# An identity matrix made on Pool, and the first K row moved ahead of the second Q row in the opening of an attention kernel

## The chip, the cores and the metric

The kernel runs on one core of one Trainium2 chip. The metric is the device time of one execution in microseconds. Each time given for a kernel is the median of several runs; one further execution was recorded by the hardware profiler, and all rows of a profile come from it.

## The reference

```
d_k = q.shape[-1]                                   # q, k, v: 8 x 2048 x 512, float32
scores = np.matmul(q, k.transpose(0, 2, 1)) / np.sqrt(d_k)
attn_weights = special.softmax(scores, axis=-1).astype(np.float32)
return np.matmul(attn_weights, v)
```

Plain attention without a mask, for 8 batches of 2048 queries and keys of width 512.

## The kernel before

The kernel casts q, k and v to 16-bit floats, brings q and k into transposed form (width on the partitions), forms transposed score tiles with TensorE, puts them through an exponential on ScalarE, and multiplies the weights with v. Most products of both matmuls are done seven for eight, by a scheme of Strassen's kind; the sums that this needs are VectorE's work. The row sums come from a column of ones next to v. All instructions are issued in an order written by hand: each engine runs its own list in that order, and strings of words (`SECOND`, `OPENING`, `SEQUENCES`) say what comes next. In the steady state, q and k are loaded by Pool with a cast into `stage` and transposed by DMA from SP.

The change lies in the opening, the first dozen microseconds, where that way would be too slow to start. There the first four rows of Q blocks and of K blocks (a "row" here is a block of 128 queries or keys by 512 numbers, 256 KB as float32) are loaded without a cast, by `load_first`. Q row 0 goes first on SP's queue, K row 0 on ACT's queue (it is the only one there besides the identity), and Q row 1, K row 1, Q row 2, K row 2, Q row 3 and K row 3 follow on SP's. `round_first` casts a row to 16 bits: Q rows on VectorE (DVE), K rows on ScalarE (ACT). `first_transpose` then transposes it on TensorE (PE), by four 128x128 transposes against an identity matrix `ident` into a PSUM tile `tr`, which DVE copies into `qraw` or `kraw`. `piece(kb, half, n, w)` multiplies K block `kb` with `w` of the Q rows from `n` on. In the profile the load is line 131, the cast line 135, the transposes line 156, their copy line 159 and the product of `piece` line 258.

`ident` lies in a corner of the tile `vt4`, which is not needed for v before much later. It comes from a constant in DRAM by a DMA that ACT issues ahead of everything else (line 95). `idle(n, name, w)` issues `n` dummy matmuls of width `w` (512 by default) on a cleared tile `warm` (line 768); they fill PE's time while it has nothing to multiply.

Behind the first rows come the other rows of the first batch. Pool loads them (`LOADS`, ten words, in the order q1, k1, q2, k2, k3, v0, v1, q3, v2, v3, where each is four rows), some of them into the places `left` and `right` that the weights use later. So that they do not take the DMA engines from the first rows, Pool first runs a one-column copy into `gate`, which reads K row 0 (line 728) and so cannot start before that row has landed. PE transposes these rows too, in `OPENING`, for which `q10v`, `k20v`, `q30v` and so on are the words (line 156 again, reading `right` or `left`).

Of the kernel before, what the change touches and what calls it, by code (L numbers as in the profile page):

```python
# [12 lines left out]
def kernel(  # L13
# [21 lines left out]
    nc = tc.nc  # L35
    P = 128
# [37 lines left out]
    def bank(name):  # L74
        t = psum[name].tile([P, 512], F32, tag=name)
        return t
# [14 lines left out]
    vt4 = const.tile([P, NJ, H], F16, name="vt4")  # L91
    ident = vt4[:, NJ - 1, 0:P]
    warm = vt2[:, 0:2, :].rearrange("p j d -> p (j d)")
    ident_dram = nc.inline_tensor(np.eye(P, dtype=np.float16), name="attn_identity")
    nc.scalar.dma_start(out=ident, in_=ident_dram.ap())
    NK = NJ // 2
    Q = H // 2
    vus = [[const.tile([P, NK, Q], F16, name=f"vu{n}_{h}") for n in (1, 2, 4)] for h in range(2)]
# [25 lines left out]
    firsts = {}  # L124
# [8 lines left out]
    def round_first(what, n):  # L133
        f = nc.vector.tensor_copy if what == "q" else nc.scalar.copy
        f(out=staged[what, 0, 0][:, n, :], in_=firsts[what, n])  # L135
# [15 lines left out]
    def transposed(what, c, n, w, copy):  # L151
        src = staged[what, 0, c]
        tr = psum["px"].tile([P, 2, ND, P], F16, tag="px", name="tr")
        for m in range(w):
            for dc in range(ND):
                nc.tensor.transpose(  # L156
                    tr[:, m, dc, :], src[:, n + m, dc * P:(dc + 1) * P], ident
                )
        copy(out=raw_of(what, 0, c)[:, n:n + w], in_=tr[:, 0:w])  # L159
        if n + w == CH:  # L160
            staged.pop((what, 0, c))
# [5 lines left out]
    def first_transpose(what, n, copy=nc.vector.tensor_copy):  # L167
        transposed(what, 0, n, 1, copy)
# [59 lines left out]
    def weights(sp, kb, half):  # L228

        left, right = pts[sp]  # L230
        j, s = divmod(kb, 2)
        if half:
            return right[:, j, 1 + s, :]
        return right[:, j, 0, :] if s else left[:, j, :]

    def exp(out_, in_):
        nc.scalar.activation(out=out_, in_=in_, func=EXP, scale=inv_sqrt_d)  # L237
# [13 lines left out]
    def piece(kb, half, n, w, last=False):  # L251

        fresh = (kb, half) not in banks
        if fresh:
            banks[kb, half] = bank(HOMES[half][kb])
        st = banks[kb, half]
        for dc in range(ND):
            nc.tensor.matmul(  # L258
                st[:, n * P:(n + w) * P], kraw[:, kb, dc, :],
                qraw[0][:, half * NT + n:half * NT + n + w, dc, :],  # L260
                start=(fresh and dc == 0), stop=(dc == ND - 1), skip_group_check=True,
            )
        if last:
            exp(weights(0, kb, half), st[:])
# [442 lines left out]
    )  # L707

    nc.vector.memset(warm, 0.0)
    nc.gpsimd.memset(vt1[:, :, H:H + 1], 1.0)  # L710
    nc.gpsimd.memset(vraw[0][:, :, 1, D:D + 1], 1.0)

# [12 lines left out]
        load_first("k", n, nc.sync, rest[n])  # L725

    gate = const.tile([P, 1], F32)
    nc.gpsimd.tensor_copy(out=gate[:], in_=firsts["k", 0][:, 0:1])

    new_p(1)  # L730
    spare = [
# [34 lines left out]
    def idle(n, name="qy", w=512):  # L766
        for _ in range(n):
            nc.tensor.matmul(
                dummies[name][:, 0:w], warm[:, 0:P], warm[:, 0:w], start=True, stop=True
            )  # L770
# [3 lines left out]
    round_first("q", 0)  # L774
    round_first("k", 0)
    first_transpose("q", 0)
    round_first("q", 1)
    round_first("k", 1)
    idle(2)
    first_transpose("q", 1)  # L780
    idle(4, "pz", P)
    first_transpose("k", 0)
    idle(6, "pz", P)
    round_first("q", 2)
    round_first("k", 2)
    piece(0, 0, 0, 1)
    first_transpose("k", 1)
    piece(0, 0, 1, 1)
    first_transpose("q", 2)
# [95 lines left out]
```

## Time and profile before

| | before |
|---|---|
| median of 3 runs | 788.87 us |
| lowest and highest | 788.74 and 789.52 us |
| the profiled execution's own time | 790.05 us |
| its span, first to last instruction | 788.2 us |
| PE busy in the span | 782.7 us (99%) |
| DVE, ACT, Pool busy | 683.8, 609.8, 72.3 us |
| HBM read and written | 100.70 and 33.55 MB |

In rows of the timeline, the first number is the start in microseconds from the start of the span, the second the length; then come the engine, the line, the operation, what is written and what is read, the shape and the count. Square brackets hold the idle time before it and what ended it. PEld is TensorE's load of weights, which can run beside a matmul; an engine's name with a q behind it stands for its queue, where DMAs are issued. "DMA to landing" is the time from the issue of a DMA to its data being there. A busy PE is not PE at its peak, since the ends of matmuls are modelled.

### The profile page before, as it was taken

To read this page: it belongs to the slowest core of one execution; us is meant where nothing else is said; L and a number is where in the kernel's file an instruction comes from. 1 tells how busy PE (TensorE), PEld (TensorE's weight loads), DVE (VectorE), ACT (ScalarE), POOL (GpSimd) and SP (SyncE) were. 2 spreads that over 40 slices of the span, in tenths; PEclk is the share of its full clock that TensorE was granted. 3 is DMA by queue.
4 is the path that set the end of the run, shared out by engine and by line. 5 is a ranking of instruction groups with operands and counts; after the bars stand their busy time and mean duration, and the time that the engine had idled before them with its cause. 6 is when DMAs were issued, how large, how long until landed. Compare 5 with 4: busy or idle time off the path is not lost.

```text
span 788.2 us, 16289 instructions
## 1 busy us (share of the span) xinstructions
PE 782.7 (99%) x6284; PEld 536.4 (68%) x6284; DVE 683.8 (87%) x1452; ACT 609.8 (77%) x1140; POOL 72.3 (9%) x105
## 2 busy tenths in 40 slices
PE   8999999999999999999999999999999999999998
PEld 6566667667667666666666666666666766766677
DVE  5799988989889898998879988799897988889884
ACT  4888788787877878878787878878788777887762
POOL 4011100011000110010100001000110001100000
PEclk9999999999999999999999999999999999999999
DMA  9999895889958889589895989958898688921113
GB/s 210 190 155 167 155 182 125 164 149 151 198 114 162 156 150 175 110 162 179 119 193 126 160 161 146 191 108 169 141 191 155 117 178 137 191 75 45 48 67 110
DMA packets 187789, 115.90 MB, mean 147 GB/s; under 512 B 121536, under 2 KB 170816, under 8 KB 187712
## 3 DMA queue, kind: packets, MB, share of 16 engines
q0 software_dynamic: 49664, 49.29, 43.7%
q1 hardware_dynamic: 137616, 65.22, 36.8%
q8 instruction: 49, 0.80, 0.4%
q10 hardware_dynamic: 432, 0.36, 0.2%
q14 instruction: 28, 0.23, 0.1%
HBM read 100.70 MB, written 33.55 MB: 170 GB/s over the span
## 4 chain that ended last, share of the span: by engine, by line
PE 97%; DMA 2%; DVE 0%; ACT 0%; issue 0%; ACTq 0%; DVEq 0%
PE t L298 46%; PE t L494 36%; PE t L418 12%; DMA kraw<-stage 1%; PE t L243 1%; PE t L258 1%; PE tr L156 1%; DMA rows<-in_k_dram 1%; PE t L566 0%; DVE kraw L159 0%; ACT rows L435 0%; DVE rows L506 0%; DVE ks L185 0%; ACT stage L135 0%; DVE cz L318 0%
## 5 line engine op out<-in xcount | busy, mean ns | idle before, releaser
L298 PE MATMUL t<-qraw,kraw 128*128 128x512 f16 x732 | 192.4, 379 | 0.0
L494 PEld LDWEIGHTS <-s 128*128 128x128 f16 x1536 | 147.8, 98 | 39.4 <-ACT rows L503 0.3
L298 PEld LDWEIGHTS <-kraw 128*128 128x128 f16 x984 | 93.3, 98 | 79.0 <-issue 0.2
L298 PE MATMUL t<-qs,ks 128*128 128x512 f16 x492 | 141.1, 379 | 0.0
L494 PE MATMUL t<-vt,s 128*128 128x257 f16 (+1 forms) x1024 | 132.9, 273 | 0.0
L237 ACT ACTIVATE right<-cz 128x1024 f16<-128x1024 f32 x123 | 129.9, 1056 | 0.3 <-DVE cz L318 0.3
L426 DVE TENSOR_TENSOR rows<-t,rows 128x256 f32<-128x256 f32 x210 | 88.1, 419 | 22.3 <-ACT rows L517 11.8
L298 PEld LDWEIGHTS <-ks 128*128 128x128 f16 x738 | 69.3, 98 | 46.7 <-issue 0.2
L503 ACT ACTIVATE rows<-t,scales 128x256 f32<-128x256 f32 x136 | 63.9, 471 | 45.2 <-PE t L494 20.9
L506 DVE SCALAR_TENSOR_TENSOR rows<-t,scales,rows 128x256 f32<-128x256 f32 (+1 forms) x134 | 64.0, 479 | 34.4 <-ACT rows L503 21.0
L321 DVE TENSOR_TENSOR cz<-t,cz 128x512 f32<-128x512 f32 x123 | 84.2, 685 | 10.5 <-ACT cz L315 7.9
L237 ACT ACTIVATE left<-t 128x512 f16<-128x512 f32 x128 | 76.5, 598 | 20.1 <-PE t L298 16.3
L237 ACT ACTIVATE right<-t 128x512 f16<-128x512 f32 x138 | 83.1, 605 | 8.5 <-PE t L298 5.7
L318 DVE TENSOR_TENSOR cz<-t,cz 128x512 f32<-128x512 f32 x123 | 84.2, 684 | 4.4 <-PE t L298 3.8
L312 ACT COPY cz<-t 128x512 f32<-128x512 f32 x122 | 71.4, 585 | 15.7 <-PE t L298 13.5
L315 ACT COPY cz<-t 128x512 f32<-128x512 f32 x123 | 71.6, 582 | 10.3 <-PE t L298 10.0
L418 PEld LDWEIGHTS <-left 128*128 128x128 f16 x960 | 62.3, 98 | 23.3 <-DVE left L398 4.1
L308 ACT COPY t<-t 128x512 f32<-128x512 f32 x121 | 69.8, 577 | 6.3 <-PE t L298 4.0
L298 PE MATMUL t<-qraw,ks 128*128 128x512 f16 x246 | 73.2, 379 | 0.0
L298 PE MATMUL t<-qs,kraw 128*128 128x512 f16 x246 | 73.2, 379 | 0.0
L494 PE MATMUL t<-vh,right 128*128 128x256 f16 x544 | 69.8, 273 | 0.0
L494 PE MATMUL t<-vh,s 128*128 128x257 f16 x512 | 66.7, 273 | 0.1
(87 smaller groups left out, 1067.1 us busy)
## 6 DMA issues: line engine op xcount, KB each, us to landing
out_dram<-rows SPq DMA_DIRECT2D x60, 512.0 KB, 3.4
vh<-in_v_dram POOLq DMA_DIRECT2D x32, 512.0 KB, 10.8
stage<-in_q_dram POOLq DMA_DIRECT2D x28, 512.0 KB, 6.5
stage<-in_k_dram POOLq DMA_DIRECT2D x28, 512.0 KB, 7.2
right<-in_k_dram POOLq DMA_DIRECT2D x2, 512.0 KB, 12.1
out_dram<-rows SPq DMA_DIRECT2D x4, 256.0 KB, 2.0
out_dram<-rows SPq DMA_DIRECT2D x7, 128.0 KB, 1.7
rows<-in_q_dram SPq DMA_DIRECT2D x2, 256.0 KB, 3.3
```

What stands on the lines that cost most here:

```text
L237: nc.scalar.activation(out=out_, in_=in_, func=EXP, scale=inv_sqrt_d)
L298: nc.tensor.matmul(dst[:], lhs[:, j, dc, :], rhs[:, :, dc, :], start=(n in (1, 5) and dc == 0), stop=(dc == 1), skip_group_check=True,)
L308: self.edges[0](out=self.y[:], in_=self.x[:])
L312: self.edges[1](out=self.cz[:, 1, :], in_=self.z[:])
L315: nc.scalar.copy(out=self.cz[:, 0, :], in_=self.x[:])
L318: nc.vector.tensor_add(self.cz[:, 1, :], self.x[:], self.cz[:, 1, :])
L321: nc.vector.tensor_add(self.cz[:, 0, :], self.z[:], self.cz[:, 0, :])
L418: nc.tensor.matmul(to, lhs[:, j, h, :], rhs[:, j, :], start=(n in (1, 2) and h == 0 and j == 0), stop=(j == NK - 1), skip_group_check=True,)
L426: nc.vector.tensor_add(acc, part, acc)
L494: nc.tensor.matmul(dst[:, 0:width], lhs(j), rhs(j), start=(first and j == 0), stop=(j == NJ - 1), skip_group_check=True,)
L503: nc.scalar.activation(out=out_, in_=src, func=COPY, scale=r)
L506: nc.vector.scalar_tensor_tensor(out=out_, in0=src, scalar=r, in1=out_, op0=MULT, op1=ADD)
```

## The change

The identity is no longer loaded: Pool clears the 128x128 corner and then sets its diagonal to one by an `affine_select`, ahead of its two other memsets. ACT's first DMA is then K row 0. The gate of Pool's loads reads K row 1 instead of K row 0. In the opening's order, the transposes of K row 0 and the first product (`piece(0, 0, 0, 1)`) stand before the cast and transposes of Q row 1 and before the cast of K row 1, and the dummies are dealt out anew.

```diff
-    ident_dram = nc.inline_tensor(np.eye(P, dtype=np.float16), name="attn_identity")
-    nc.scalar.dma_start(out=ident, in_=ident_dram.ap())
...
     nc.vector.memset(warm, 0.0)
+    nc.gpsimd.memset(ident, 0.0)
+    nc.gpsimd.affine_select(
+        out=ident, in_=ident, compare_op=mybir.AluOpType.not_equal, fill=1.0,
+        base=0, pattern=[[-1, P]], channel_multiplier=1,
+    )
     nc.gpsimd.memset(vt1[:, :, H:H + 1], 1.0)
     nc.gpsimd.memset(vraw[0][:, :, 1, D:D + 1], 1.0)
...
     gate = const.tile([P, 1], F32)
-    nc.gpsimd.tensor_copy(out=gate[:], in_=firsts["k", 0][:, 0:1])
+    nc.gpsimd.tensor_copy(out=gate[:], in_=firsts["k", 1][:, 0:1])
...
     round_first("q", 0)
     round_first("k", 0)
     first_transpose("q", 0)
+    idle(1)
+    first_transpose("k", 0)
     round_first("q", 1)
     round_first("k", 1)
-    idle(2)
+    idle(4, "pz", P)
+    piece(0, 0, 0, 1)
+    idle(4, "pz", P)
     first_transpose("q", 1)
-    idle(4, "pz", P)
-    first_transpose("k", 0)
-    idle(6, "pz", P)
+    idle(2, "pz", P)
     round_first("q", 2)
     round_first("k", 2)
-    piece(0, 0, 0, 1)
     first_transpose("k", 1)
     piece(0, 0, 1, 1)
```

## The prediction

> **What bounds the kernel now.** The page comes first, for the engine that the chain of waits runs through.
>
> ```profile
> PE 782.7 (99%) x6284; PEld 536.4 (68%) x6284; DVE 683.8 (87%) x1452; ACT 609.8 (77%) x1140; POOL 72.3 (9%) x105
> PE 97%; DMA 2%; DVE 0%; ACT 0%; issue 0%; ACTq 0%; DVEq 0%
> ```
>
> PE is busy for 99% of the span and carries 97% of the chain. An edit that only reorders the opening can win what PE stands idle there, and no more. The windows view says where that idle time lies (columns: stretch, length, busy time and count of PE, PEld, DVE, ACT, POOL, granted clock, DMA share, GB/s).
>
> ```profile
> 0.00:9.12 9.12, 6.92 (x46) 3.49 (x46) 3.16 (x9) 3.09 (x5) 3.07 (x11) 1.00 0.74 237
> 9.12:60.00 50.88, 50.88 (x383) 31.89 (x384) 41.39 (x92) 38.73 (x67) 10.73 (x16) 1.00 1.16 176
> 60.00:400.00 340.00, 339.88 (x2718) 232.24 (x2717) 303.35 (x641) 270.63 (x510) 31.87 (x43) 1.00 0.88 155
> 400.00:780.00 380.00, 380.00 (x3089) 264.32 (x3088) 333.02 (x709) 296.03 (x557) 26.68 (x36) 1.00 0.72 135
> ```
>
> From 9.12 to 780 us PE is idle for 0.12 us of 770.88. Before 9.12 it is idle for 2.20, and part of its 6.92 busy is dummy matmuls. So whatever moves the matmul at 9.12 moves the end by as much, as long as nothing later holds PE up. The chain in order of time says what puts that matmul at 9.12 (start, length, what):
>
> ```profile
> 1.13 5.24 DMA rows<-in_k_dram
> 6.37 0.02 issue
> 6.39 0.63 ACT stage L135
> 7.02 0.05 issue
> 7.07 0.41 PE tr L156 x4
> ...
> 7.50 0.44 DVE kraw L159
> ...
> 8.38 0.24 PE tr L156 x4
> ...
> 8.64 0.43 DVE kraw L159
> 9.08 0.05 issue
> 9.12 0.61 PE t L258 x4
> ```
>
> K row 0, sent by ACT at 1.13, lands at 6.37; cast, transposes and copy follow, and after them the copy of K row 1 at 8.64 releases the matmul at 9.12 (K block 1 against the first two Q rows). The steps around this, from the timeline:
>
> ```profile
> 0.73 0.37 ACTq L95 DMA_DIRECT2D vt<-attn_identity  x1
> 0.74 0.87 SPq L131 DMA_DIRECT2D rows<-in_q_dram  x2
> 3.58 0.43 DVE L135 CAST stage<-rows 128x512 f16<-128x512 f32 x1 [2.45 <-DMA rows<-in_q_dram]
> 4.06 0.61 PE L156 MATMUL tr<-vt,stage 128*128 128x128 f16 x4
> 4.46 1.06 PE L768 MATMUL t<-vt 128*128 128x512 f16 x2
> 4.71 0.42 DVE L159 COPY qraw<-tr 128x512 f16<-128x512 f16 x1 [0.70 <-PE tr L156]
> 5.05 0.42 DVE L135 CAST stage<-rows 128x512 f16<-128x512 f32 x1
> 5.92 0.52 PE L768 MATMUL t<-vt 128*128 128x128 f16 x4
> 7.07 0.40 PE L156 MATMUL tr<-vt,stage 128*128 128x128 f16 x4 [0.63 <-ACT stage L135]
> 7.84 0.49 DVE L135 CAST stage<-cz 128x512 f16<-128x512 f32 x1
> ```
>
> Step lengths from these rows: cast to transpose 0.48 (3.58 to 4.06); transpose to its copy 0.65 in the early stretch (4.06 to 4.71) and 0.43 later (7.07 to 7.50); two DVE operations back to back 0.34 (4.71 to 5.05); copy to the matmul that needs it 0.48 (8.64 to 9.12); four transposes 0.40 of PE (4.06 to 4.46) and one 512-wide dummy 0.53 (half of 1.06).
>
> **The change part by part.** *The identity.* The DMA at 0.73 goes. ACT then issues K row 0 at about 0.73 instead of 1.13: 0.40 earlier. Pool gets a memset and a select of 128x128 ahead of its other two memsets; the transpose of Q row 0 waits for them. No Pool operation of that size is in the trace; the nearest rows are these:
>
> ```profile
> L710 POOL MEMSET vt<- 128x8 f16 x1 | 0.1, 133 | 0.3 <-POOLq L869 0.3
> L869 POOL MEMSET const-float32-1.0<- 128x1 f32 x1 | 0.1, 99 | 0.0
> L805 POOL CAST gate<-qraw 128x1 f32<-128x1 f16 x1 | 0.7, 696 | 21.1 <-DMA qraw<-right 21.1
> ```
>
> From 1 to 8 columns the time grows by 34 ns, about 5 per column; 128 columns would be 0.13 + 120 x 0.005 = 0.73 us. Two of them from 0.73 end at 2.2. The bounds are 2 x 0.10 (ready at 0.93) and two operations each twice that estimate (ready at 3.65). Even the upper one lies ahead of the transpose at 4.06. I take 2.2 and a cost of nothing: the cover is Q row 0's flight and cast. If the cover fails, every step below moves with the identity.
>
> *K row 0 beside Q row 0.* It now flies together with Q row 0 instead of behind it. Q row 0 alone, and the rate of the DMA engines while both queues are full:
>
> ```profile
> DMA to landing us min/median/max: 2.8/2.8/2.8
> 2.50:3.00 0.50, 0.50 (x3) 0.22 (x2) 0.00 (x0) 0.42 (x1) 0.00 (x0) 1.00 1.01 357
> ```
>
> At 357 GB/s another 256 KB takes 0.73. If the two share evenly, both land at 0.74 + 2.8 + 0.73 = 4.27: Q row 0 later by 0.73 than now (3.54), K row 0 earlier by 2.1. Bounds: neither pays for the other (3.5), and K row 0 flies as long as now (0.73 + 5.24 = 5.97). The DMA share of 1.01 in that row shows the engines full before K row 0 moves at all. Behind that row stands a rule that speaks against this edit: the Trainium skill, "DMA: Bandwidth & Descriptors", section "Issuing engines are not separate DMA queues", says that transfers started from different engines end up on the same 16 DMA engines and interleave. By it the even split is right and Q row 0 pays; were the queues separate, both rows would land at 3.5.
>
> *The order on PE and DVE.* New order: transposes of Q row 0, one dummy, transposes of K row 0, four small dummies, first product, four small dummies, transposes of Q row 1, two small dummies, and then K row 1 as before. On DVE the cast of Q row 1 now stands behind the copy of K row 0, and the copy of Q row 1 and the cast of Q row 2 stand behind that: this is the wait that the change adds. With Q row 0 at 4.27: its transposes at 4.27 + 0.02 + 0.48 = 4.77; then 0.40 and the dummy's 0.53, so K row 0's transposes at 5.70 (its own data are there at 4.27 + 0.70 = 4.97). Copy of K row 0 at 5.70 + 0.65 = 6.35; cast of Q row 1 at 6.69; its transposes at 7.17, its copy at 7.60, cast of Q row 2 at 7.94, copy of K row 1 0.36 behind at 8.30 (0.34, and a little for the longer cast of 0.49), the matmul of 9.12 at 8.78. That is 0.34 us earlier. K row 1 doesn't hold this up:
>
> ```profile
> L131 SPq DMA_DIRECT2D rows<-in_k_dram x1: 424/424/424, 1.7 to 1.7; - x1
> DMA to landing us min/median/max: 4.9/4.9/4.9
> ```
>
> It lands at 1.66 + 4.9 = 6.56 (issue at 1.7 in the row, 1.66 in the timeline), is cast by about 7.2 and transposed behind Q row 1. The removed dummies, 2 wide of 0.53 now against 1, and as many small ones as before, 10, are filler whose place is in the steps above.
>
> *The gate.* Pool's loads of the later rows wait for K row 1 instead of K row 0: 6.56 instead of 6.37 if K row 1 lands as now. K row 1 has the same bytes ahead of it as now less the identity's 32 KB (0.09 us at 357 GB/s), so I put it at 6.47, 0.10 later than the gate opens now. Queued behind the gate are all of Pool's first loads. Those loads are nearly just in time (issue from the first rows, PE's use from the last two pairs):
>
> ```profile
> L121 POOL DMA_DIRECT2D right<-in_k_dram x1: 785/785/785, 10.2 to 10.2; - x1
> DMA to landing us min/median/max: 11.2/11.2/11.2
> L121 POOL DMA_DIRECT2D left<-in_q_dram x1: 820/820/820, 13.2 to 13.2; - x1
> DMA to landing us min/median/max: 21.7/21.7/21.7
> 21.60 0.65 PEld L156 LDWEIGHTS <-right 128*128 128x128 f16 x8
> 21.81 0.61 PE L156 MATMUL tr<-vt,right 128*128 128x128 f16 x8
> 35.04 0.65 PEld L156 LDWEIGHTS <-left 128*128 128x128 f16 x8
> ```
>
> K rows 8 to 11 land at 10.23 + 11.2 = 21.43 (10.23 is the issue in the timeline) and their weights are loaded at 21.60; PE uses them at 21.81, and one weight load takes 0.10, so PE waits as soon as it is more than 21.81 - 0.10 - 21.43 = 0.28 early. The Q rows land at 13.16 + 21.7 = 34.86 against 35.04, with 0.18 or, by the same allowance, 0.28. So of the 0.34 won at 9.12 about 0.28 passes these two places if the loads land as now. A gate 0.10 later need not move them: from 9.12 to 60 the DMA share is 1.16, full engines, and the landing then follows from the bytes moved, which are 32 KB fewer. I take no shift, with bounds of 0.2 either way.
>
> **Sum.** 0.34 won, cut to 0.28, say 0.3. The profiled execution took 790.05 us in all (its span 788.2), so it would be 789.75; against the median of 788.87, which is 1.18 below it, 788.6. That is 0.04%; about 0.2% (1.6 us) is what a measurement of this kernel can tell from no change.
>
> **The rivals.** *K row 0 still comes late (slower).* The old order had Q row 1 cast while K row 0 was still flying; the new one makes DVE wait for it. From K row 0's transposes to the matmul is 8.78 - 5.70 = 3.08, so the break-even is transposes at 6.04, which is K row 0 landing at 5.34, or Q row 0 at 4.61. For it: the flight of 5.24 now, nearly twice Q row 0's. Against it: that flight began behind the identity and with two Q rows in the queue. At 5.97 the matmul comes at 5.97 + 0.70 + 3.08 = 9.75, 0.63 later, and with nothing to give it back the time is 789.5.
>
> *The gain is hidden by the loads.* K row 1 as now, the gate 0.19 later and the loads later by as much: 0.28 - 0.19 = 0.1 is left, 788.8.
>
> *More than forecast.* Q row 0 hardly delayed and the loads 0.2 to 0.4 earlier, because the queue drains sooner: 0.5 to 0.8, 788.2.
>
> *TensorE's clock comes up later (slower).* Four transposes keep the next matmul waiting 0.40 at 4.06 but 0.24 in the chain at 8.38, and their row falls from 0.61 at 4.06 to 0.40 at 7.07, behind small dummies that still take 0.52 for four at 5.92: PE is slower until between 6.4 and 7.1, some 5.5 us after its first matmul, which follows the clearing of the dummies' tile at 1.2. The new order widens the hole ahead of Q row 0's transposes from 0.1 to 0.8 us (its six first dummies last until 3.9; the transposes come at 4.77). If that began the count anew, the faster clock would come at 4.77 + 5.5 = 10.3, and the dense work from 8.78 on would lose 0.4 of 1.5 (1 - 0.24 / 0.40), with 0.2 for the slower steps ahead: 0.8 - 0.34, so 0.5 slower, 789.4. Against it: the wait of 0.63 before 7.07 does no harm now. The Trainium skill, "TensorE: Matmul & The Clock Gate", section on the HAM clock gate, says that the fast clock follows a window of about 3.4 us of sustained work and that the windows run free of the kernel's start; by it one hole could cost a window or nothing.
>
> *The identity is late (slower).* It decides if it is ready after 5.1: transposes 0.05 later, K row 0's 0.93 later, and 3.08 to the matmul make 4.06, and 9.12 - 4.06 is 5.06. At 7.3 it would cost 2.2 us, 791.1; no Pool row above comes near that. The Trainium skill, "GPSIMD Engine Reference", section "Instruction dispatch", gives about 6 us for the first call of a freshly loaded Pool kernel; by it the identity would come near 7.3. No operation in this trace shows such a start.
>
> **How the numbers follow.** Forecast 0.40; hidden 0.18; more than forecast 0.14; K row 0 late 0.14; clock late 0.07; identity late 0.07. Faster than 787.3 takes both the largest bounds of the third case: 0.05 of its 0.14, and 0.01 for the unforeseen, 0.06. Slower than 790.4 needs the late identity (0.07) or a late K row 0 and a late clock together (0.04): 0.11. The rest, 0.83, is within 0.2%. The range takes the hidden gain, the late row and the late clock above, and the larger gain below, with 0.2 for the load bounds and 0.3 for the spread of the runs shown (788.74 to 789.52): 787.8 to 789.9.
>
> **What would show it.** Right: no DMA by ACT but K row 0 at the start; Pool done with the identity before 3.6; Q row 0 landing near 4.3 and K row 0 with it; K row 0's transposes near 5.7; the two-row matmul of K block 1 near 8.8; the weight loads at 21.60 no longer early but waiting for the DMA. Wrong: K row 0 landing beyond 5.3, transposes of 0.61 after 7.1, PE's first transpose waiting for Pool, or idle time of PE beyond the opening.

## The result, and the profile after

| | before | after |
|---|---|---|
| median | 788.93 us, 16 runs | 790.64 us, 16 runs |
| lowest and highest | 788.60 and 789.74 | 789.50 and 792.37 |
| ratio | | 1.0022, 95% interval 1.0015 to 1.0030 |

The change costs 1.7 us. The forecast was a gain of 0.3, with a range up to 789.9.

The windows view of the changed kernel (columns as before) shows part of it: PE's idle time grew from 2.20 to 3.10 before 9.12, and by 0.53 between 60 and 400; elsewhere it hardly changed. That is 1.43 of the 2.3 us by which the two spans differ; of the rest, 0.7 is busy time of PE (783.4 for 782.7). The 0.53 belongs to this one execution: in a second profile of the changed kernel, below, PE was busy for 340.00 of these 340 us.

```profile
0.00:9.12 9.12, 6.02 (x33) 3.48 (x34) 1.88 (x5) 3.18 (x5) 3.41 (x13) 1.00 0.78 235
60.00:400.00 340.00, 339.35 (x2713) 231.71 (x2712) 302.98 (x640) 270.69 (x509) 31.87 (x43) 1.00 0.87 155
400.00:780.00 380.00, 379.99 (x3083) 263.69 (x3082) 333.06 (x708) 296.53 (x559) 26.68 (x36) 1.00 0.73 134
```

The timeline of the same execution has the rows that answer to those quoted in the prediction (the lines of the loads, casts, transposes and products have moved by two, that of the gate by three):

```profile
0.73 0.39 ACTq L129 DMA_DIRECT2D rows<-in_k_dram  x1
0.73 0.20 POOL L708 MEMSET vt<- 128x128 f16 x1 [0.29 <-POOLq L873]
1.01 0.29 POOL L709 TENSOR_SCALAR_AFFINE_SELECT vt<-vt 128x128 f16<-128x128 f16 x1
...
5.09 0.62 ACT L133 CAST stage<-rows 128x512 f16<-128x512 f32 x1 [2.65 <-DMA rows<-in_k_dram]
5.27 0.43 DVE L133 CAST stage<-rows 128x512 f16<-128x512 f32 x1 [4.14 <-DMA rows<-in_q_dram]
5.75 0.61 PE L154 MATMUL tr<-vt,stage 128*128 128x128 f16 x4 [1.82 <-DVE stage L133]
...
6.52 0.18 POOL L731 COPY gate<-rows 128x1 f32<-128x1 f32 x1 [5.11 <-DMA rows<-in_k_dram]
...
10.09 0.63 PE L154 MATMUL tr<-vt,stage 128*128 128x128 f16 x4
10.52 0.64 PE L256 MATMUL t<-qraw,kraw 128*128 128x256 f16 x4
11.00 0.39 PE L154 MATMUL tr<-vt,stage 128*128 128x128 f16 x4
```

Three things are to be seen. The identity is ready at 1.3. Q row 0, not K row 0, is the last to land: its cast starts at 5.27, where it started at 3.58, so TensorE idles 1.82 us ahead of its first transposes. And four transposes take 0.61 to 0.63 until 10.09 and 0.39 at 11.00: the faster clock came some 4 us later than before. (The clock column of the windows view doesn't show this, it reads 1.00 in the opening too; the part on the hole and the clock has the trace's record of it.) The matmul of K block 1 with two Q rows (the "two-row matmul" below) comes at 10.52, before it came at 9.12.

This execution was the slowest of the 16, and the one profiled of the kernel before, 790.05, was slower than all 16 of its runs. So each kernel was profiled a second time. The kernel before, 788.73 us, span 787.0:

```profile
3.78 0.43 DVE L135 CAST stage<-rows 128x512 f16<-128x512 f32 x1 [2.65 <-DMA rows<-in_q_dram]
5.11 1.26 ACT L135 CAST stage<-rows 128x512 f16<-128x512 f32 x2 [2.19 <-DMA rows<-in_k_dram]
5.14 0.19 POOL L728 COPY gate<-rows 128x1 f32<-128x1 f32 x1 [4.24 <-DMA rows<-in_k_dram]
5.25 0.41 DVE L135 CAST stage<-rows 128x512 f16<-128x512 f32 x1
8.22 0.61 PE L258 MATMUL t<-qraw,kraw 128*128 128x256 f16 x4
```

The changed kernel, 790.87 us, span 789.0:

```profile
4.98 0.43 DVE L133 CAST stage<-rows 128x512 f16<-128x512 f32 x1 [3.85 <-DMA rows<-in_q_dram]
5.47 0.61 PE L154 MATMUL tr<-vt,stage 128*128 128x128 f16 x4 [1.54 <-DVE stage L133]
6.29 0.63 PE L154 MATMUL tr<-vt,stage 128*128 128x128 f16 x4
8.28 0.63 PE L154 MATMUL tr<-vt,stage 128*128 128x128 f16 x4
8.95 0.42 DVE L157 COPY qraw<-tr 128x512 f16<-128x512 f16 x1 [1.22 <-PE tr L154]
10.14 0.61 PE L256 MATMUL t<-qraw,kraw 128*128 128x256 f16 x4
```

In an ordinary execution of the kernel before, K row 0 lands at 5.1, not at 6.4, and the two-row matmul comes at 8.22. In the changed kernel it comes at 10.14. That is 1.92 of the 2.0 by which the two spans differ: nearly the whole loss is made in the first ten microseconds.

### The profile page after: what moved, and what is told of

Its sections match the earlier page's. It is cut to its first block, busy times and chain, and to the rows that moved or that the text cites. A ratio compares the mean times of both kernels' runs of the same rounds, so it can differ in the third digit from the quotient of the medians.

```text
span 790.5 us, 16290 instructions
## 1 busy us (share of the span) xinstructions
PE 783.4 (99%) x6283; PEld 537.6 (68%) x6283; DVE 683.1 (86%) x1452; ACT 610.0 (77%) x1140; POOL 72.3 (9%) x107
## 4 chain that ended last, share of the span: by engine, by line
PE 97%; DVE 1%; ACT 1%; DMA 1%; issue 0%; DVEq 0%
PE t L296 46%; PE t L492 36%; PE t L416 12%; PE t L241 1%; PE t L256 1%; PE tr L154 1%; DMA rows<-in_q_dram 1%; ACT right L235 0%; DVE cz L319 0%; DVE rows L504 0%; DVE rows L424 0%; PE t L771 0%; ACT rows L501 0%; ACT rows L433 0%; DVE cz L316 0%
```

## The experiments

Three theories stood at the start. **A**: two first rows that start together delay Q row 0. **B**: the hole that TensorE is left with delays its faster clock. **C**: the new order costs, because VectorE's work on Q row 1 waits for K row 0. Two more came up: **D**, the later gate costs, and **E**, the first profile of the kernel before was of an unusual execution. Each kernel was timed beside the kernel before on the same chip. The table gives, of the one execution profiled, when the cast of Q row 0 and of K row 0 began, the start of the two-row matmul, and the start of the last four transposes that took over 0.5 us.

| kernel | median (range), us | before there | Q row 0 | K row 0 | two-row | slow until |
|---|---|---|---|---|---|---|
| before, first and second profile | | | 3.58; 3.78 | 6.39; 5.11 | 9.12; 8.22 | 5.52; 4.26 |
| after, first and second profile | 790.64 | 788.93 | 5.27; 4.98 | 5.09; 5.15 | 10.52; 10.14 | 10.09; 8.91 |
| e1 identity alone | 790.78 (789.69-791.79) | 789.0 | 4.89 | 5.08 | 9.13 | none |
| e2 order alone | 790.19 (789.36-790.58) | 789.0 | 3.61 | 5.09 | 9.61 | 8.36 |
| e3 after, hole filled | 789.87 (789.62-790.33) | 789.0 | 4.93 | 4.75 | 8.80 | none |
| e4 after, K row 0 on SP | 790.80 (790.07-791.67) | 789.0 | 3.46 | 4.06 | 8.81 | 4.77 |
| e5 after, old gate | 790.92 (789.62-791.68) | 789.18 | 5.18 | 5.02 | 9.05 | none |
| e6 before with a hole | 790.27 (789.27-791.37) | 789.18 | 3.97 | 5.13 | 9.58 | 9.15 |
| e8 after, filled, old gate | 790.17 (789.57-790.74) | 789.18 | 4.67 | 4.84 | 9.46 | 5.43 |
| e9 after, K row 0 on SP, old gate | 789.36 (788.82-789.89) | 788.83 | 3.48 | 4.15 | 8.71 | 3.96 |
| e10 identity alone, stand-in DMA | 789.14 (788.62-789.59) | 788.83 | 3.62 | 5.34 | 8.08 | none |
| e11 order alone, filled | 789.58 (789.35-790.28) | 788.83 | 3.68 | 5.18 | 8.93 | 4.16 |
| e12 before, filled | 788.88 (788.31-789.24) | 788.83 | 3.53 | 5.29 | 8.31 | 5.63 |
| e13 identity alone, K row 0 issued later | 789.15 (788.46-790.54) | 789.15 | 3.44 | 4.84 | 8.51 | 6.22 |
| e14 after, stand-in DMA | 790.35 (789.28-790.96) | 789.15 | 3.92 | 5.24 | 8.94 | 4.40 |
| e15 identity alone, K row 0 on SP | 790.74 (788.76-790.91) | 789.15 | 3.53 | 4.15 | 9.80 | 8.65 |

**The parts apart.** e1 is the changed kernel with the old order and the old gate; e2 is the kernel before with the new order.

```diff
# e1, against the changed kernel: gate on firsts["k", 0], and
-    idle(1)
-    first_transpose("k", 0)
     round_first("q", 1)
     round_first("k", 1)
-    idle(4, "pz", P)
-    piece(0, 0, 0, 1)
-    idle(4, "pz", P)
+    idle(2)
     first_transpose("q", 1)
-    idle(2, "pz", P)
+    idle(4, "pz", P)
+    first_transpose("k", 0)
+    idle(6, "pz", P)
     round_first("q", 2)
     round_first("k", 2)
+    piece(0, 0, 0, 1)
# e2, against the kernel before: the same lines the other way round
```

> The identity made on Pool and K row 0 first on ACT's queue, but the old order and the old gate. Theory A (the two first rows start together and Q row 0 pays for it: it landed at 5.25 instead of 3.54): Q row 0 lands near 5.2 here too, its transposes start near 5.7 instead of 4.06, and the time is 0.8 to 1.7 us above the kernel before. Rival B (the transfers matter only through the hole on TensorE that keeps its clock low: four transposes in 0.61 until 10.9 instead of until 7): the hole is the same here, so slow transposes beyond 9 and the same time as under A. Rival C (the new order is what costs, since VectorE's cast of Q row 1 waits behind K row 0): within 0.3 us of the kernel before.

> The new order alone: identity loaded by DMA and old gate as in the kernel before. Theory A: Q row 0 lands at 3.5 again; K row 0 lands at about 6.4, behind the loaded identity, so its copy comes at 7.5, the cast of Q row 1 at 7.8 and the matmul that stood at 9.12 at about 9.9, 0.8 us slower than before. Rival B: the new wait for K row 0 (5.5 to 7.07) is a hole as well and the clock may come up a window later: slow transposes beyond 8 and 1.3 to 2 us slower. Rival C: slower by as much as the whole change, 1.7 us, without slow transposes after 8.

e1: 1.0020 (1.0011 to 1.0029) of the kernel before; e2: 1.0010 (1.0001 to 1.0018). Each part alone costs, by the medians 1.8 and 1.2 us (by the ratios 1.6 and 0.8), so C alone is refuted by e1, and the parts do not add up: the whole change costs 1.7. In e1 Q row 0 is late as A says:

```profile
4.89 0.43 DVE L133 CAST stage<-rows 128x512 f16<-128x512 f32 x1 [3.76 <-DMA rows<-in_q_dram]
```

The execution of e1 that was profiled took 789.69 us, the least of its 11, and its transposes took 0.40 from the first on, so B's "slow transposes beyond 9" were not seen. With the fast clock its two-row matmul still comes at 9.13, 0.91 behind 8.22. Its other ten runs are slower; that their clock came late is likely but not recorded. In e2 Q row 0 is early again (3.61), and the clock is late. K row 0 was cast at 5.09 there, where 6.4 was expected.

**What delays Q row 0.** Three kernels change only how K row 0 is sent, in e1:

```diff
# e10: in front of K row 0 on ACT's queue, a DMA that nothing reads
+    unused = vt4[:, NJ - 2, 0:P]
+    unused_dram = nc.inline_tensor(np.eye(P, dtype=np.float16), name="attn_unused")
+    nc.scalar.dma_start(out=unused, in_=unused_dram.ap())
# e13: in front of it, no DMA, but a copy of one column on ACT
+    early = const.tile([P, 1], F32)
+    nc.scalar.copy(out=early[:], in_=vt1[:, 0, H:H + 1])
# e15 (and e4, in the changed kernel): K row 0 behind Q row 0 on SP's queue
-    load_first("k", 0, nc.scalar, row(1))
+    load_first("k", 0, nc.sync, row(1))
```

> The identity made on Pool, old order, old gate, and ahead of K row 0 on ACT's queue a stand-in of the removed DMA (32 KB into a place that nothing reads). Theory A: K row 0 starts behind Q row 0 again, Q row 0 lands at 3.5 to 3.8, and the time is that of the kernel before, 789.0 within 0.4, against 790.8 without the stand-in. If the identity on Pool itself costs (or ACT's earlier start): 790.4 or more.

> The identity made on Pool, old order, old gate, no stand-in; ahead of K row 0's DMA ACT copies one column, so that its table load and this copy come first and the DMA is issued near 2.1 instead of 0.73. If Q row 0 pays for a second queue that starts at the same moment (theory A): Q row 0 lands at 3.4 to 3.8 again, K row 0 at 5.2 to 5.8, and the time is 788.8 to 789.5. If the small packets of the removed DMA were what helped: Q row 0 lands at 4.7 or later as without the stand-in, and the time is 790.4 or more.

> The identity made on Pool, old order, old gate, K row 0 on SP's queue behind Q row 0. Theory A: Q row 0 lands at 3.4, K row 0 at 4.0, Q row 1 only near 5.5 to 5.9, so the old order's transposes of Q row 1 come at 6.4, those of K row 0 behind them at 6.8 and the matmul of K block 1 with two Q rows at 8.4 to 8.7; 788.8 to 789.3, level with the kernel before. A better kernel than before only if Q row 1 lands by 5: 788.3 to 788.6.

Both e10 and e13 give the time of the kernel before: 1.0000 (0.9991 to 1.0009) and 0.9998 (0.9990 to 1.0007). The identity on Pool is therefore free within the 0.7 us that the intervals leave, and what costs 1.8 in e1 is K row 0 starting at the same moment as Q row 0, with the hole that Q row 0's delay leaves on TensorE. e13 settles what it is about the stand-in that helps: without any small packets, an issue at 1.41 instead of 0.73 is enough (it came earlier than the 2.1 expected, beside ACT's table load).

```profile
1.41 0.38 ACTq L129 DMA_DIRECT2D rows<-in_k_dram  x1
3.44 0.43 DVE L133 CAST stage<-rows 128x512 f16<-128x512 f32 x1 [2.31 <-DMA rows<-in_q_dram]
4.84 1.30 ACT L133 CAST stage<-rows 128x512 f16<-128x512 f32 x2 [2.62 <-DMA rows<-in_k_dram]
```

So with K row 0 sent 0.68 later Q row 0 lands 1.4 earlier than in e1 (3.44 against 4.89), and K row 0 no later (cast at 4.84; at 4.75 to 5.15 in the six profiles in which both start together). The stretch from 2.0 to 3.5 shows the difference (last two columns: DMA share, GB/s). The kernel before in its second profile, and e13:

```profile
2.00:3.50 1.50, 1.50 (x5) 0.46 (x3) 0.00 (x0) 0.92 (x1) 0.00 (x0) 1.00 0.82 280
```

```profile
2.00:3.50 1.50, 1.50 (x5) 0.44 (x3) 0.06 (x1) 0.20 (x2) 0.00 (x0) 1.00 0.92 317
```

The changed kernel in its second profile, and e1:

```profile
2.00:3.50 1.50, 1.50 (x5) 0.45 (x3) 0.00 (x0) 0.45 (x1) 0.00 (x0) 1.00 0.92 210
```

```profile
2.00:3.50 1.50, 1.50 (x5) 0.45 (x3) 0.00 (x0) 0.46 (x1) 0.00 (x0) 1.00 0.92 172
```

The engines are as busy, but move 172 and 210 GB/s instead of 280 and 317: the two rows do not share a full rate, they lower it. The rates of this stretch lie apart in all profiles: 158 to 227 GB/s in the six with both rows sent together, 251 to 317 in the twelve others. e15 misses: Q row 0 is early, but Q row 1 now stands behind both, its cast starts at 5.79, and TensorE waits for it. Seven of its eleven runs gather at 790.7 to 790.9, among them the one profiled, whose clock is late; four lie at 788.8 to 789.6.

**The hole and the clock.** e3 fills the hole ahead of the first transposes, e6 makes one in the kernel before, e12 adds a dummy to the kernel before; e11 fills what the order alone leaves open.

```diff
# e3, in the changed kernel        # e6, e12, in the kernel before
-    idle(5)                       -    idle(5)
+    idle(9)                       +    idle(1)      # e12: idle(6)
# e11, in e2
-    idle(1)
+    idle(3)
     first_transpose("k", 0)
```

> The changed kernel with four more wide dummies ahead of Q row 0's transposes (9 instead of 5), so that TensorE is busy until Q row 0 is cast. Rival B: four transposes take 0.40 instead of 0.61 from about 7 on instead of from 10.9 on, the matmul on K block 1 and the first two Q rows comes at 9.5 to 9.8 instead of 10.5, and the time falls by 0.7 to 1.1 us against the changed kernel, to 789.6 to 789.9. Theory A without B: Q row 0's landing is unchanged and so is the time, 790.6 within 0.3.

> The kernel before with one wide dummy instead of five behind the first: TensorE stands idle from about 2.0 until Q row 0's transposes at 4.06; DMAs and order are those of before. Theory B: the faster clock comes one count later, four transposes take 0.61 until 9 or later in most executions, and the time rises by 0.5 to 1.4 us, to 789.5 to 790.4. If holes do not matter: 789.0 within 0.3.

> The new order alone (old DMAs, old gate), with two more wide dummies between the transposes of Q row 0 and of K row 0, where the new order left TensorE idle from 5.1 to 5.8. Theory B (the order's cost is mostly a clock that comes up late): the runs gather at the lower of the two values that the order alone gave, 789.4, and few at 790.2. Rival C (the order costs because VectorE's work for Q row 1 waits for K row 0): the median stays at 790.0 to 790.3.

> The kernel before with one more wide dummy ahead of Q row 0's transposes. In the second profile of the kernel before TensorE was idle from 3.93 to 4.26 there. Theory B: some executions of the kernel before get their clock a window late for this hole, the spread upward shrinks, and the median falls by 0.1 to 0.4 us, to 788.6 to 788.9. If that hole never decides: 789.1 within 0.2, or 0.1 later.

B holds in size. e3 is 0.77 below the changed kernel, with Q row 0 hardly earlier (4.93), and transposes of 0.40 from the first on; its two-row matmul, at 8.80, came earlier than the 9.5 to 9.8 expected. e6 loses 1.1 with the DMAs and the order of the kernel before:

```profile
4.46 0.61 PE L156 MATMUL tr<-vt,stage 128*128 128x128 f16 x4 [2.24 <-DVE stage L135]
...
9.15 0.63 PE L156 MATMUL tr<-vt,stage 128*128 128x128 f16 x4
9.58 0.65 PE L258 MATMUL t<-qraw,kraw 128*128 128x256 f16 x4
10.06 0.39 PE L156 MATMUL tr<-vt,stage 128*128 128x128 f16 x4
```

e11 brings the order alone from 1.19 above the kernel before beside it to 0.75: its runs gather at 789.35 to 789.85, one at 790.28, where those of e2 fell into four at 789.4 and seven at 790.1 to 790.6. The remaining 0.75 is read as C, and the rows agree: the two-row matmul is 0.71 behind 8.22, and Q row 1's cast, at 5.25 in the kernel before, waits behind the copy of K row 0.

```profile
6.29 0.42 DVE L159 COPY kraw<-tr 128x512 f16<-128x512 f16 x1 [1.05 <-PE tr L156]
6.63 0.49 DVE L135 CAST stage<-rows 128x512 f16<-128x512 f32 x1
8.93 0.61 PE L258 MATMUL t<-qraw,kraw 128*128 128x256 f16 x4
```

e12 gave nothing, 1.0000 (0.9991 to 1.0009): the holes of 0.13 and 0.33 us in the two profiles of the kernel before are harmless.

Each trace also has a record of the clock that TensorE was granted; it begins with the full clock, and that beginning settles B. The record gives 6.18 and 5.02 us in the two profiles of the kernel before, 10.59 and 9.26 in those of the changed kernel, 9.66 in e6, and 4.01 to 5.11 where the table says "none". The stretches of full clock last 778.24, 781.65 or 785.07 us, so they differ by steps of 3.41. In the step of 3.41 us that ends where the full clock begins, TensorE's matmuls, as the trace has them, fill 80% or more in all 18 traces; in the step ahead of that one, 76% or less. For the changed kernel that earlier step, with the hole in it, is 47% and 55% full. Where these steps lie against the kernel's start differs from run to run, and the six dummies ahead of the hole last 2.74 us, 80% of a step. In e1, e5 and e10 one step held all six, and the clock was up by 4.3, hole or no hole.

The Trainium skill, "TensorE: Matmul & The Clock Gate", section on the HAM clock gate, says that the windows in which the clock is judged run free of the kernel. The traces agree: the opening of e5, with TensorE idle from 3.9 to 5.67, had its transposes at 0.40 from 5.67 on, with the full clock from 4.14; the changed kernel, with the same opening but for the gate, had them at 0.63 until 10.09. The runs of e5 fall into two groups that fit this, three at 789.6 to 789.7 and eight at 790.6 to 791.7; of these only the fastest was profiled.

**The gate.**

```diff
# e5, in the changed kernel; e8, in e3; e9, in e4
-    nc.gpsimd.tensor_copy(out=gate[:], in_=firsts["k", 1][:, 0:1])
+    nc.gpsimd.tensor_copy(out=gate[:], in_=firsts["k", 0][:, 0:1])
```

> The changed kernel with the gate of Pool's loads back on K row 0. Theory D (the gate costs of itself, since the loads start a micro second later than behind K row 0's landing at 5.1): 0.5 us or more faster than the changed kernel, 790.1 or less. Theory B (cold clock): in the changed kernel TensorE is late by more than the loads, no wait for a load shows in its trace, so the gate hides: 790.6 within 0.3.

> The changed kernel with nine wide dummies (the hole filled) and the gate back on K row 0. With the hole filled alone the matmul of K block 1 with two Q rows came at 8.80, but TensorE then waited 1.3 and 0.4 us for Pool's loads. Theory D: those waits go with the older gate, and the time falls by 0.5 to 1 us from 789.87, to 788.9 to 789.4. If the late loads come from the DMA engines being full and not from the gate: 789.9 within 0.3.

> The changed kernel with K row 0 issued by SP right behind Q row 0, nothing on ACT's queue. Theory A: Q row 0 lands near 3.5 and K row 0 near 4.9, the hole is gone, the clock is up by 7, the matmul on K block 1 and the first two Q rows comes near 8.7 and the time is 788.5, at or 0.4 us under the kernel before. If the slow first transfers have nothing to do with two queues starting at once: Q row 0 lands near 5 as in the changed kernel and the time is 790 or more. Rival C: the new order costs its share even with an early Q row 0, 789.5 or more.

> The changed kernel with K row 0 on SP's queue behind Q row 0 and the gate back on K row 0. With the first of these alone Q row 0 landed at 3.4, K row 0 at 4.0, and TensorE then waited about 2 us for Pool's loads, whose gate opened only at 7.25. Theory A: with the gate open at 4.1 those waits go, and the time is 788.5 to 789.3, no slower than the kernel before. If the DMA engines are the limit whatever the gate: 790 or more, with waits for the loads, or for the first rows that the loads now compete with.

> The whole changed kernel (new order, gate on K row 1) with the 32 KB stand-in ahead of K row 0 on ACT's queue. The order alone gave 790.19, so if the early K row 0 is undone and the gate costs nothing: 790.2 within 0.3. If the later gate costs as well once TensorE is early enough to wait for loads: 790.5 or more, with waits for loads in the trace. If the parts make good for each other: under 789.9.

The gate's share depends on the rest. In the changed kernel it is hidden: e5 at 790.92 is no faster than 790.64, and in the profile of the changed kernel TensorE waits for none of Pool's loads. Where TensorE is early it shows. e4 was expected at 788.5 and took 790.80. In it both first rows land early (cast at 3.46 and 4.06), but the gate opens at 7.25, and PEld waits for Pool's loads (line, what for: us in total, times, longest):

```profile
PEld L154 <- DMA right<-in_k_dram: 1.3, 1, 1.3
PEld L154 <- DMA right<-in_q_dram: 0.4, 1, 0.4
PEld L154 <- DMA left<-in_q_dram: 0.3, 1, 0.3
```

With the gate back on K row 0, open at 4.18, e9 takes 789.36 instead of 790.80 (0.53 instead of 1.80 above the kernel before beside it, just over the 789.3 expected), and the waits shrink:

```profile
PEld L154 <- DMA left<-in_q_dram: 0.6, 1, 0.6
PEld L154 <- DMA right<-in_k_dram: 0.5, 1, 0.5
```

e3 waits for the loads as well, but e8, with its gate open at 4.87, took 790.17 against 789.87 (each about 0.9 to 1.0 above the kernel before beside it): D's expected gain of 0.5 to 1 did not come. Its trace has no such waits, but a two-row matmul at 9.46 instead of 8.80, behind casts on VectorE of 0.55 and 0.65 instead of 0.42 and transposes still slow at 5.43. Whether early loads lengthen those casts was not tried apart. e14, at 790.35, shows that order and gate lose 1.2 with Q row 0's landing mended (3.92). That is as much as the order alone lost in e2, and its trace has no wait for a load: the later gate added nothing there.

**The second profiles.**

> The kernel before, unchanged, for a second profile. Theory E (the first profile was of an unusual execution, in which one DMA engine delivered its share of K row 0 over a micro second late; the order alone, with the same DMAs, showed K row 0 at 5.07): K row 0 lands at 5.0 to 5.2, the matmul that stood at 9.12 comes at 7.9 to 8.4, Pool's loads start at 5.2, the span is about 787.2. If the first profile was typical: K row 0 near 6.4, the matmul near 9.1, span 788.2.

> The changed kernel, unchanged, for a second profile. Theory A: Q row 0 lands at 4.6 to 5.3 again. Theory B: if the time is 790.3 or more, four transposes still take 0.61 at 8; if it is near 789.6, they take 0.40 from 7 on. If the first profile's opening was peculiar: Q row 0 lands under 4.5, and 790.6 needs another cause.

E holds, and the changed kernel's second profile shows what A and B expected of it: Q row 0 cast at 4.98, and four transposes still at 0.63 at 8.28. Eight profiles have the DMAs of the kernel before up to K row 0, or the stand-in in the identity's place (the kernel before twice, e2, e6, e10, e11, e12, e14). K row 0's cast began at 5.09 to 5.34 in seven of them and at 6.39 in the one that the prediction was made from. There, of the sixteen signals with which this DMA reports that its data have landed, fifteen came by 5.16 and the last at 6.37; in the second profile all came by 5.09. No version beat the kernel before: e10, e12 and e13 are level with it.

## Why the prediction was wrong, step by step

**What bounds the kernel** was right: the end follows the two-row matmul, and 1.92 of a difference of 2.0 between the spans lie there.

**The chain that put it at 9.12** was read rightly, but of an unusual execution. This is the first step that failed. The 5.24 us of K row 0 was the size on which the gain rested; it is 3.9 to 4.2 in the other seven. The hint was on the page: the profiled execution lay 1.18 above the median. The prediction carried that over as a constant, where most of it was the late row: the second profile has the matmul 0.90 and the span 1.2 earlier. So there was nothing to win: the two-row matmul stands at 8.22, 0.56 ahead of the 8.78 that the prediction worked out for the changed kernel.

**The identity** was right: ready at 1.3, inside the bounds and ahead of the 2.2 taken, and it cost nothing that e10 and e13 can tell.

**K row 0 beside Q row 0** is the step that failed next, by size. Taken was an even split of 357 GB/s, both rows at 4.27. In the six profiles with both rows sent together (the changed kernel twice, e1, e3, e5, e8) the cast of Q row 0 began at 4.67 to 5.27 (3.58 and 3.78 before), and that of K row 0 at 4.75 to 5.15. So Q row 0 was 0.9 to 1.7 late where 0.73 was taken, and K row 0, taken as 2.1 earlier, was hardly earlier than its ordinary 5.09 to 5.34. The bound "neither pays" was far off, and the upper one stood for K row 0 only: none was set for Q row 0. The rule of the Trainium skill, "DMA: Bandwidth & Descriptors", section "Issuing engines are not separate DMA queues", that the transfers interleave on the same DMA engines pointed the right way. The lower rate from 2.0 to 3.5 goes beyond it.

**The order**: with Q row 0's cast at 4.98 the prediction's own steps give K row 0's transposes at 4.98 + 0.48 + 0.93 = 6.39 and the matmul 3.08 later, at 9.47; they came at 6.29 and 10.14. Against 8.22 that is 1.25 for the late row and the order, and 0.67 for steps at the slow clock. The wait of VectorE that the prediction named is there without the late row too: e11, 0.75.

**The rivals.** "K row 0 comes late" had the right place, DVE's queue, and a break-even for Q row 0 (4.61, counted from the late 9.12), but gave it to the wrong row. "The clock comes up later" was priced at 0.8 ahead of the gain, rightly, since filling the hole was worth 0.77; but it was given 0.07, and its sign, transposes of 0.61 after 7.1, is in both profiles of the changed kernel. It counted the clock from the first matmul; the records show no such count, the full clock came 2.8 to 9.4 us after it. A late row and a late clock came together; the prediction gave that 0.04.

**The gate** was put 0.10 later than before; against an ordinary execution of the kernel before it is 1.3 later (6.4 for 5.1). In the changed kernel that is hidden.

## What to carry to other kernels

Set the profiled execution's own time against the runs before reading a stall off it: a microsecond above the median may be an event of that execution, and the gain counted on it may not exist in the others. When two engines' queues send the first transfers, let the one that is needed first start alone; here 0.7 us of delay for the second made the first land 1.4 us earlier and the second no later. An opening that makes the first real matmul wait can cost twice, once for the wait and once for the clock that comes later.

## What the runs showed of the hardware

With two transfers of 256 KB started together from two queues, 158 to 227 GB/s were moved from 2.0 to 3.5 us, where 280 and 317 were moved with the second issued 0.4 and 0.7 later; what slows the packets was not found. TensorE's full clock began at 4.14 us in one profile and at 10.59 in another, in openings that differ in nothing but the gate. In all 18 traces it began at the end of a stretch of 3.41 us that matmuls filled to 80% or more, and the stretch ahead of that was filled to 76% or less. With a hole of 1.7 us the late case was the more frequent one, if the eight higher runs of e5's eleven are read so. Pool's memset of 128x128 took 0.20 and its select 0.29, less than the 0.73 estimated from narrow memsets.
